# Twelve of sixteen k-tiles of the attention's input products in seven-product form instead of ten

## The chip, the cores and the metric

The kernel runs on one core of one Trainium2 chip. The metric is the device time of one execution in microseconds (us). The kernel before takes 1580.58 us (median of three runs, 1579.58 to 1581.96).

## The reference

A two-layer encoder for 256 tokens of width 2048. Layer 1 is a Mamba-2 mixer. Layer 2 is a forgetting attention with 32 heads of 128. The change touches only the products that make q, k, v and z of layer 2:

```python
def forgetting_attention_mixer(h, w_in, b_forget, w_out):
    proj = h @ w_in                       # h: 256 x 2048
    q = proj[..., :E_WIDTH]               # E_WIDTH = 4096, the same for k, v, z
    ...
    o = o * jax.nn.silu(z)
    return o @ w_out
```

Everything is float32. A float32 product is made of three products of a faster type: each operand is split in a high part and a low remainder, and high*high, high*low and low*high are added up.

## The kernel before, in words

**Splitting the weights.** Each weight tile of 128 x 1024 is loaded (by SP, the engine that issues most loads). ScalarE rounds it into `wh` (`act_hi`, L106), and VectorE subtracts to get the remainder `wl` (`dve_lo`, L112). TensorE multiplies both with the activations (`product`, L132). `prep` (L140) does this for plain weights, `prep_sum` (L172) for weights that are sums. `run` (L209) walks a list of parts. Before the matmuls of a part are emitted, the preparation of the part three places further on (`AHEAD`) is emitted. There are five buffers for `wh`, four for `wl`, and seven (`RAW`) of 128 x 1024 for loaded tiles, the tag `raw`.

**Blocks.** Layer 2 goes over eight groups of four heads (`hq`, `four_heads`, L1136). Each group has two blocks: the first makes q and k, the second v and z. A block multiplies the 256 x 2048 input with a left and a right half of 512 columns. The 2048 rows are 16 k-tiles of 128. With two token tiles, two column halves and pairs of k-tiles, the product is one of 2 x 2 blocks, so it can be made with seven products instead of eight (Winograd's form of Strassen's scheme). This needs sums of the input blocks (`split_form`, L282: seven matrices of 128 x 128 for a pair of k-tiles, held in `forms`) and sums of the weight blocks.

**Sums of weights.** `wf_s` holds, for a set of four k-tiles (two pairs side by side, 128 x 1024), four terms. Three chains run in place. Chain a is term 0, then term 1 is added (A1), then chain b (A3), then term 2 (A2). Chain b is term 3 (B0), then term 1 is added (B1). Chain c is term 2 alone (C0). Each of these seven states is split and multiplied once: six matmuls of 512 columns. Adding a term from memory is done by a DMA that accumulates, issued by GpSimd (POOL, L198). Adding chain b to chain a is done by VectorE (L200).

**What is in sums.** For groups 1 to 7, ten of the sixteen k-tiles (`KS`) are in that form: two sets of four, and a third set of only two k-tiles (`pairs` is 1), 512 wide, from `wf_h`. For the third set, term 1 is loaded once, as `term` (L188, L189), and VectorE adds it to chain a (L196) and to chain b (L193), so one DMA accumulates there, A2. The other six k-tiles are multiplied directly: three tiles `raw` each for the left ("L") and right ("R") columns, twelve matmuls each (`mm_rest`, L1065). Group 0 keeps two sets and four L and four R tiles in each of its blocks, because the forms of the later k-tiles aren't there yet; `late_form` (L952) makes the fifth pair of forms during group 0's second block.

**Order.** `STEPS` (L1019) gives the order of a block of groups 1 to 7: A0 and the other names stand for three parts, one for each set. `FIRST` and `SECOND` are the orders of group 0. After the two blocks of groups 1 to 5 come eight parts (12 matmuls each) of the output projection of the group before (`out_f`, L1355, timed at 22.8 us); the blocks of groups 6 and 7 follow each other without one. The attention of a group itself (transposes, logits, softmax, values) is spread over the parts that follow its second block (`later`, L125).

**Where sums live.** Sums of the first two sets are in `raw` buffers, but chain b of the first set is in a tile `sum` of its own (`apart`). The third set's chains a and b take the sixth buffers of the forms' tags (`gh`, `gl`), changing places from block to block, and c a `raw` buffer. `x3` is the tile that holds k-tiles 10 and 11 of the input; after group 0 the input is still read from `x3` directly by L and R parts. `zth` is a pair of 128 x 512 buffers, used by the gate among others. All instructions of an engine run in the order in which the program lists them, SP's loads and POOL's DMA issues too.

Of the kernel before, what the change touches and what calls it, by code (L numbers as in the profile page):

```python
# [45 lines left out]
KS = 10  # L46
# [23 lines left out]
def hybrid_kernel(ctx: ExitStack, tc: tile.TileContext, a):  # L70
# [101 lines left out]
    def prep_sum(u):  # L172


        name, src, how = u["chain"]
        wide = u.get("wide", 1024)
        if how == "load":
            if u.get("apart"):
                t = fp[0].tile([P, 1024], F32, tag="sum", name=f"sum_{name}")
            elif wide < 1024 and name != "c":  # L180
                t = gp.tile([P, 7, P], F32, tag="gh" if (name == "a") == u["even"] else "gl",
                            name=f"sum_{name}").rearrange("p m s -> p (m s)")
            else:
                t = wp.tile([P, 1024], F32, tag="raw", name=f"sum_{name}", bufs=RAW)
            u["sums"][name] = t[:, :wide]
            nc.sync.dma_start(u["sums"][name], src)
            if wide < 1024 and name == "c":
                u["sums"]["t"] = t = fp[0].tile([P, wide], F32, tag="term", name="term")  # L188
                nc.sync.dma_start(t, u["term"])  # L189
        elif how == "add" and "term" in u:  # L190
            t = u["sums"]["t"]
            if name == "b":
                nc.vector.tensor_tensor(t, t, u["sums"]["b"], op=ALU.add)  # L193
                u["sums"]["b"] = t
            else:
                nc.vector.tensor_tensor(u["sums"][name], u["sums"][name], t, op=ALU.add)  # L196
        elif how == "add":
            behind["POOL"] = nc.gpsimd.dma_start(u["sums"][name], src, accum_op=ALU.add).ins  # L198
        else:
            nc.vector.tensor_tensor(u["sums"][name], u["sums"][name], u["sums"][how], op=ALU.add)  # L200
        raw = u["sums"][name]
        wh = wp.tile([P, 1024], F32R, tag="wh", name="wh")[:, :wide]
        wl = wp.tile([P, 1024], F32R, tag="wl", name="wl", bufs=4)[:, :wide]
        act_hi(wh, raw)
        behind["DVE"] = dve_lo(wl, raw, wh).ins
        u["w"][0] = (wh, wl)
        yield
# [161 lines left out]
    def ktile(x, k):  # L369

        q = max(i for i in range(5) if X_AT[i] <= k)
        return x[q][:, k - X_AT[q]]
# [579 lines left out]
    def late_form():  # L952

        f = fp[0].tile([P, T2, 1024], F32, tag="vz", name="form", bufs=2)
        f = f.rearrange("p t c -> p (t c)")[:, :7 * P].rearrange("p (m s) -> p m s", m=7)
        for i in range(2):
            hi, lo = (ktile(lay2["x"], KS0 + i)[:, j].rearrange("p (t s) -> p t s", t=T2)
                      for j in range(2))
            nc.vector.tensor_tensor(blocks(f, True, i), hi, lo, op=ALU.add)
        split_form(f, True, lay2["forms"], 0, f"x{KS0 // 2}")  # L960
# [58 lines left out]
    STEPS = (A0, C0, "L", B0, "L", A1, "L", A3, "R", "R", "R", B1, A2)  # L1019
    SECOND = (A0, C0, "L", B0, "L", "L", A1, "L", A3, "R", "R", "R", B1, A2, "R")  # L1020
    FIRST = (0, "L", "L", 1, "L", A0, C0, B0, "L", "enter", A1, A3, "R", "R", "R", B1, A2, "R")

    def block_units(w_s, w_p, out, scale, done, order):
# [7 lines left out]
        pairs = (2, 2, 1)[:len(w_s)]  # L1031
        n_l = KT - 2 * len(w_p[0])
        steps = [0]
# [20 lines left out]
        def mm_sum(u, form, name, p2):  # L1054
            wh, wl = u["w"][0]
            first = start(name)
            for i, w in enumerate((wh, wh, wl)):
                for p in range(pairs[p2]):
                    y = lay2["forms"][0][2 * p2 + p][i % 2]
                    product(ps[name], y[:, form, :], w[:, p * 512:p * 512 + 512],  # L1060
                            start=first and i == p == 0,
                            stop=i == 2 and (p2, p + 1) == (len(pairs) - 1, pairs[-1]),
                            skip_group_check=True)
# [31 lines left out]
        for step in order[0]:  # L1095
# [6 lines left out]
            if step in n_rest:  # L1102
                n = n_rest[step]
                n_rest[step] += 1
                names = ("v", "y") if step == "L" else ("z", "u")
                u = us[step]
                parts.append({"u": u, "h": [n],
                              "mm": lambda u=u, n=n, names=names: mm_rest(u, n, names)})
                if n + 1 == len(u["w"]) and step == "L":
                    parts[-1]["post"] = left if order[0] is not SECOND else (  # L1110
                        lambda: [left(), later(1, late_form)])
                continue
            chain, term, how, form, name = step
            for p2 in range(len(pairs)):
                u = {"chain": (chain, w_s[p2][term], how), "sums": sums[p2], "w": [None],
                     "wide": 512 * pairs[p2], "even": order[2],
                     "apart": chain == "b" and p2 == 0 and order[0] is not FIRST}
# [18 lines left out]
    def four_heads(hq, first=()):  # L1136
# [139 lines left out]
        def weights(n):  # L1276
            s1, s2 = a["wf_s"][hq, n], a["wf_h"][hq, n]
            half = lambda c, m: a["wf_p"][hq, n, c][:, m * 1024:m * 1024 + 1024]
            rest = [[half(c, m) for m in range((KT - KS) // 2)] for c in range(2)]
            if hq == 0:  # L1280
                return [s1[0], s1[1]], [[a["wf_b"][n, c], *rest[c]] for c in range(2)]
            return [s1[0], s1[1], s2], rest
# [92 lines left out]
def packed(x, norm_w, m_w_in, m_conv_w, m_conv_b, m_dt_bias, m_A_log, m_D,  # L1375
# [21 lines left out]
    def tiles_b(left, right):  # L1397

        w = np.stack([left.reshape(D, G, 512), right.reshape(D, G, 512)], 2)
        s = w[:KS0 * P].reshape(KS0 // 4, 2, 2, P, G, 2, 512).transpose(4, 0, 2, 5, 3, 1, 6)
        h = w[KS0 * P:KS * P].reshape(2, P, G, 2, 512).transpose(2, 0, 3, 1, 4)
        r = w[KS * P:].reshape(KT - KS, P, G, 2, 512).transpose(2, 3, 1, 0, 4)
        b = w[KS0 * P:KS * P, 0].reshape(2, P, 2, 512).transpose(2, 1, 0, 3)
        return (f(s).reshape(G, KS0 // 4, 4, P, 1024), f(h).reshape(G, 4, P, 512),
                f(r).reshape(G, 2, P, (KT - KS) * 512), f(b).reshape(2, P, 1024))

# [18 lines left out]
    def by_k(w):  # L1428
# [13 lines left out]
        "wf_s": np.stack([qk[0], vz[0]], 1), "wf_h": np.stack([qk[1], vz[1]], 1),  # L1442
        "wf_p": np.stack([qk[2], vz[2]], 1), "wf_b": np.stack([qk[3], vz[3]]),
# [19 lines left out]
```

## Time and profile before

| what | value |
|---|---|
| median of three runs | 1580.58 us |
| the profiled execution: its own time, its span | 1580.13 us, 1578.4 us |
| blocks of group 2 (874.3 to 918.8 and 918.8 to 962.4 us) | 44.5 and 43.6 us |
| the eight output parts behind them (962.4 to 985.2) | 22.8 us |
| blocks of groups 6 and 7 (1317.9 to 1495.1) | 44.5, 43.6, 45.5, 43.6 us |
| POOL, the engine with the least work | 178.1 us (11%) |

The page gives busy times of the engines: PE is TensorE's matmuls, PEld its weight loads, DVE VectorE, ACT ScalarE, POOL GpSimd, SP the engine that issues loads. "DMA share" in a table of stretches is the packet time summed over the core's 16 DMA engines and divided by 16 times the stretch; where two packets overlap on an engine, it can pass 1. A row of a group of instructions has the count, then busy time in us, mean ns of one, and the idle time before them with what ended it.

### The profile page before, as it was taken

The numbers are of one execution on the slowest core, as the hardware profiler recorded it, in microseconds if no ns is written. First come the engines' busy times: TensorE is split into PE (matmuls) and PEld (weight loads), VectorE is DVE, ScalarE is ACT, GpSimd is POOL, SyncE is SP. The second block draws the span as 40 slices with busy tenths as digits, with TensorE's granted clock in tenths as the row PEclk, the third lists the DMA queues.
The fourth block names the chain that finished last, engine by engine and source line by source line (L and its number), as shares of the span: only waits on it lengthen the run. The fifth ranks groups of instructions, "written<-read, shape, count | busy, mean of one in ns | idle before, by whom it ended". The sixth has DMA issues, their size and how long they took to land.

```text
span 1578.4 us, 22860 instructions
## 1 busy us (share of the span) xinstructions
PE 1566.1 (99%) x7768; PEld 1320.7 (84%) x7768; DVE 1377.8 (87%) x2061; ACT 1087.1 (69%) x1710; POOL 178.1 (11%) x225
## 2 busy tenths in 40 slices
PE   9999999999999999999999999999999999999997
PEld 7888888888888888878888888888888888888886
DVE  6998989798989898799888898888888888989886
ACT  7677676767666765766776675776676675777764
POOL 0000111011100110011101110110110111011100
PEclk9999999999999999999999999999999999999999
DMA  9665798769886987579889788788886986899852
GB/s 363 211 204 197 183 275 220 262 177 277 220 271 171 274 227 230 182 170 279 241 250 286 181 239 269 219 230 262 222 262 210 258 271 165 249 276 249 251 175 80
DMA packets 106405, 364.54 MB, mean 231 GB/s; under 512 B 12176, under 2 KB 13072, under 8 KB 106160
## 3 DMA queue, kind: packets, MB, share of 16 engines
q1 hardware_dynamic: 79344, 270.03, 48.5%
q0 software_dynamic: 26800, 92.91, 30.8%
q8 instruction: 61, 1.00, 0.2%
q14 instruction: 56, 0.46, 0.1%
q10 hardware_dynamic: 144, 0.13, 0.0%
HBM read 360.83 MB, written 2.20 MB: 230 GB/s over the span
## 4 chain that ended last, share of the span: by engine, by line
PE 97%; DVE 1%; issue 0%; DMA 0%; ACT 0%; SPq 0%; ACTq 0%; POOLq 0%; POOL 0%
PE psa L132 24%; PE pst L132 17%; PE psx L132 14%; PE psz L132 10%; PE psv L132 9%; PE psu L132 8%; PE psy L132 8%; PE py L715 2%; PE pqk L1182 1%; PE psc L1200 1%; PE ppt L1232 1%; PE po L1258 0%; PE psc L1198 0%; PE pxa L665 0%; PE pyt L778 0%; PE pz L1237 0%
## 5 line engine op out<-in xcount | busy, mean ns | idle before, releaser
L112 DVE TENSOR_TENSOR wl<-raw,wh 128x1024 fp32r<-128x1024 f32 (+2 forms) x343 | 411.8, 1211 | 51.7 <-issue 21.0
L106 ACT ACTIVATE wh<-raw 128x1024 fp32r<-128x1024 f32 (+2 forms) x343 | 356.5, 1052 | 144.0 <-PE psa L132 53.8
L106 ACT ACTIVATE wh<-sum_a 128x1024 fp32r<-128x1024 f32 (+1 forms) x232 | 220.1, 953 | 132.0 <-PE psu L132 36.8
L112 DVE TENSOR_TENSOR wl<-sum_a,wh 128x1024 fp32r<-128x1024 f32 (+1 forms) x232 | 250.2, 1091 | 14.6 <-PE psa L132 5.0
L132 PE MATMUL pst<-x,wh 128*128 128x512 f32 (+1 forms) x800 | 204.3, 396 | 0.9 <-DVE wh L161 0.7
L132 PEld LDWEIGHTS pst<-x,wh 128*128 128x128 f32 (+1 forms) x800 | 145.7, 189 | 30.5 <-ACT x L108 1.4
L132 PE MATMUL psa<-wh,x 128*128 128x512 f32 x512 | 128.7, 391 | 0.0
L112 DVE TENSOR_TENSOR wl<-sum_b,wh 128x1024 fp32r<-128x1024 f32 (+1 forms) x102 | 115.1, 1146 | 5.8 <-ACT wh L106 3.9
L106 ACT ACTIVATE wh<-sum_b 128x1024 fp32r<-128x1024 f32 (+1 forms) x102 | 100.1, 1004 | 26.6 <-PE psa L132 10.5
L132 PEld LDWEIGHTS pst<-x,wl 128*128 128x128 f32 x768 | 106.3, 191 | 9.0 <-DVE wl L112 0.7
L132 PEld LDWEIGHTS psa<-wh,x 128*128 128x128 f32 x512 | 95.5, 188 | 19.7
L132 PE MATMUL pst<-x,wl 128*128 128x256 f32 x768 | 109.3, 283 | 0.0
L198 POOL DMA_DIRECT2D sum_a<-in_wf_s x64 | 55.4, 865 | 407.9 <-DMA raw<-in_wf_p 103.5
L132 PE MATMUL psz<-wh,x 128*128 128x512 f32 x200 | 78.6, 393 | 0.0
L132 PE MATMUL psv<-wh,x 128*128 128x512 f32 x200 | 78.1, 391 | 0.0
L132 PE MATMUL psu<-wh,x 128*128 128x512 f32 x200 | 78.0, 390 | 0.0
L132 PE MATMUL psy<-wh,x 128*128 128x512 f32 x200 | 77.9, 390 | 0.0
L132 PE MATMUL psx<-wh,ghx 128*128 128x512 f32 x234 | 77.7, 399 | 0.0
L106 ACT ACTIVATE wh<-sum_c 128x1024 fp32r<-128x1024 f32 (+1 forms) x58 | 54.5, 954 | 31.8 <-PE psa L132 17.4
L132 PE MATMUL psx<-wh,glx 128*128 128x512 f32 x234 | 75.9, 390 | 0.0
L132 PE MATMUL psx<-wl,ghx 128*128 128x512 f32 x234 | 75.6, 390 | 0.0
L816 DVE TENSOR_TENSOR xs<-psa,xs 128x512 f32<-128x512 f32 (+1 forms) x81 | 51.9, 679 | 22.6 <-PE psa L132 22.2
(365 smaller groups left out, 3390.3 us busy)
## 6 DMA issues: line engine op xcount, KB each, us to landing
raw<-in_wf_p SPq DMA_DIRECT2D x96, 512.0 KB, 5.2
raw<-in_wm_t SPq DMA_DIRECT2D x90, 512.0 KB, 5.1
raw<-in_wm_z SPq DMA_DIRECT2D x64, 512.0 KB, 5.6
sum_a<-in_wf_s POOLq DMA_DIRECT2D x64, 512.0 KB, 8.5
raw<-in_wf_o SPq DMA_DIRECT2D x64, 512.0 KB, 5.8
sum_a<-in_wm_s POOLq DMA_DIRECT2D x36, 512.0 KB, 5.9
sum_a<-in_wf_s SPq DMA_DIRECT2D x32, 512.0 KB, 6.7
sum_c<-in_wf_s SPq DMA_DIRECT2D x32, 512.0 KB, 9.3
```

Of the source, the lines that this page charges most:

```text
L106: nc.scalar.activation(out, in_, AF.Copy)
L112: return nc.vector.tensor_tensor(out, in_, hi.bitcast(F32), op=ALU.subtract)
L132: behind["PE"] = nc.tensor.matmul(*args, **kw).ins
L198: behind["POOL"] = nc.gpsimd.dma_start(u["sums"][name], src, accum_op=ALU.add).ins
L715: nc.tensor.matmul(st["py"][t][:, c], m[:, j, t, :], st["xd"][:, t, c], start=True, stop=True)
L816: nc.vector.tensor_tensor(c, pss[t][:, a:b], c, op=ALU.add)
L1182: nc.tensor.transpose(pt[:, n * P:n * P + P], st["qk"][:, t, c:c + FD], ident)
L1200: nc.tensor.matmul(ps[:, P:P + S], q[:, :P], k[:, P:], start=j == 0, stop=j == 2)
L1232: nc.tensor.transpose(pt[:, c:c + P], uu[:, c:c + P], ident)
```

## The change

The third set gets four k-tiles, as the first two have, so twelve of sixteen k-tiles are in sums for groups 1 to 7, and four are multiplied directly (two L and two R parts).

- All seven states of the third set are 1024 wide, with six matmuls instead of three. Two `raw` tiles (one L, one R) of each block go.
- In the third set term 1 is added to chain a by an accumulating DMA of POOL. To chain b it is added by VectorE, in two instructions of 512 columns, from two tiles (`term` and a `zth` buffer). `wf_h` goes; all sums come from `wf_s`.
- Chain b of the first set returns to the `raw` buffers (except in group 0's second block). The third set's chains a and b live in `x3` and `sum`, changing places from block to block.
- The order of a block becomes A0 C0 B0 L A1 A3 L R R B1 A2.
- `late_forms` makes two more pairs of forms (k-tiles 8 to 11) instead of one. In group 0's second block the last R goes ahead of A2. Group 0's direct tiles are the same in number.

```diff
-KS = 10
+KS = 12
...
         if how == "load":
-            if u.get("apart"):
-                t = fp[0].tile([P, 1024], F32, tag="sum", name=f"sum_{name}")
-            elif wide < 1024 and name != "c":
-                t = gp.tile([P, 7, P], F32, tag="gh" if (name == "a") == u["even"] else "gl",
-                            name=f"sum_{name}").rearrange("p m s -> p (m s)")
+            if "place" in u:
+                t = (bp if u["place"] == "x3" else fp[0]).tile(
+                    [P, 1024], F32, tag=u["place"], name=f"sum_{name}")
             else:
                 t = wp.tile([P, 1024], F32, tag="raw", name=f"sum_{name}", bufs=RAW)
...
+            if "term" in u:
+                u["sums"]["t"] = ts = (fp[0].tile([P, 512], F32, tag="term", name="term"),
+                                       sp.tile([P, 512], F32, tag="zth", name="term"))
+                for i, t in enumerate(ts):
+                    nc.sync.dma_start(t, u["term"][:, i * 512:(i + 1) * 512])
         elif how == "add" and "term" in u:
-            t = u["sums"]["t"]
-            if name == "b":
-                nc.vector.tensor_tensor(t, t, u["sums"]["b"], op=ALU.add)
-                u["sums"]["b"] = t
-            else:
-                nc.vector.tensor_tensor(u["sums"][name], u["sums"][name], t, op=ALU.add)
+            for i, t in enumerate(u["sums"]["t"]):
+                c = u["sums"][name][:, i * 512:(i + 1) * 512]
+                nc.vector.tensor_tensor(c, c, t, op=ALU.add)
...
-    def late_form():
+    def late_forms():
-        f = fp[0].tile([P, T2, 1024], F32, tag="vz", name="form", bufs=2)
-        f = f.rearrange("p t c -> p (t c)")[:, :7 * P].rearrange("p (m s) -> p m s", m=7)
-        for i in range(2):
...
+        v = fp[0].tile([P, T2, 1024], F32, tag="vz", name="form", bufs=2)
+        for q in range(KS0 // 2, KS // 2):
+            f = v[:, q % 2, :7 * P].rearrange("p (m s) -> p m s", m=7)
+            for i in range(2):
...
-    STEPS = (A0, C0, "L", B0, "L", A1, "L", A3, "R", "R", "R", B1, A2)
-    SECOND = (A0, C0, "L", B0, "L", "L", A1, "L", A3, "R", "R", "R", B1, A2, "R")
+    STEPS = (A0, C0, B0, "L", A1, A3, "L", "R", "R", B1, A2)
+    SECOND = (A0, C0, "L", B0, "L", "L", A1, "L", A3, "R", "R", "R", B1, "R", A2)
...
-                for p in range(pairs[p2]):
+                for p in range(2):
...
-                if pairs[p2] == 1 and (chain == "c" or term == 1):
-                    u["term"] = w_s[p2][1]
-                steps[0] += pairs[p2] == 1
-                parts.append({"u": u, "h": [0], "long": 1 if pairs[p2] == 2 else steps[0] % 2,
+                if order[0] is SECOND and chain == "b" and p2 == 0:
+                    u["place"] = "sum"
+                if p2 == 2:
+                    if chain == "c" or (chain, term) == ("b", 1):
+                        u["term"] = w_s[p2][1]
+                    if chain != "c":
+                        u["place"] = "x3" if (chain == "a") == order[2] else "sum"
+                parts.append({"u": u, "h": [0], "long": 1,
```

The host's packing follows: `wf_s` has three sets of four terms for each block, `wf_p` two direct tiles for each column half, `wf_b` k-tiles 8 to 11 for group 0.

More of the change, by code (lines that the diff above doesn't have):

```diff
@@ L175, in prep_sum @@
         name, src, how = u["chain"]
[L176 removed]
         if how == "load":
[L178 to L182 removed]
+            if "place" in u:
+                t = (bp if u["place"] == "x3" else fp[0]).tile(
+                    [P, 1024], F32, tag=u["place"], name=f"sum_{name}")
             else:
                 t = wp.tile([P, 1024], F32, tag="raw", name=f"sum_{name}", bufs=RAW)
[L185 to L189, printed above, removed]
[L190 to L196 removed]
+            u["sums"][name] = t
+            nc.sync.dma_start(t, src)
+            if "term" in u:
[3 more added lines that the diff above has]
+                    nc.sync.dma_start(t, u["term"][:, i * 512:(i + 1) * 512])
+        elif how == "add" and "term" in u:
+            for i, t in enumerate(u["sums"]["t"]):
+                c = u["sums"][name][:, i * 512:(i + 1) * 512]
+                nc.vector.tensor_tensor(c, c, t, op=ALU.add)
         elif how == "add":
@@ L201, in prep_sum @@
         raw = u["sums"][name]
-        wh = wp.tile([P, 1024], F32R, tag="wh", name="wh")[:, :wide]
-        wl = wp.tile([P, 1024], F32R, tag="wl", name="wl", bufs=4)[:, :wide]
+        wh = wp.tile([P, 1024], F32R, tag="wh", name="wh")
+        wl = wp.tile([P, 1024], F32R, tag="wl", name="wl", bufs=4)
         act_hi(wh, raw)
@@ L950, in form_x @@
             split_form(lay2["f"][q], True, lay2["forms"], 0, f"x{q}")
-    def late_form():
-        f = fp[0].tile([P, T2, 1024], F32, tag="vz", name="form", bufs=2)
-        f = f.rearrange("p t c -> p (t c)")[:, :7 * P].rearrange("p (m s) -> p m s", m=7)
-        for i in range(2):
[L957 to L960, printed above, removed]
+    def late_forms():
[3 more added lines that the diff above has]
+            for i in range(2):
+                hi, lo = (ktile(lay2["x"], 2 * q + i)[:, j].rearrange("p (t s) -> p t s", t=T2)
+                          for j in range(2))
+                nc.vector.tensor_tensor(blocks(f, True, i), hi, lo, op=ALU.add)
+            split_form(f, True, lay2["forms"], 0, f"x{q}")
     def stats2():
@@ L1061, in mm_sum @@
                             start=first and i == p == 0,
-                            stop=i == 2 and (p2, p + 1) == (len(pairs) - 1, pairs[-1]),
+                            stop=i == 2 and (p2, p) == (len(w_s) - 1, 1),
                             skip_group_check=True)
@@ L1108, in block_units @@
                               "mm": lambda u=u, n=n, names=names: mm_rest(u, n, names)})
+                if n + 1 == len(u["w"]) and step == "R" and order[0] is SECOND:
+                    parts[-1]["post"] = right
                 if n + 1 == len(u["w"]) and step == "L":
                     parts[-1]["post"] = left if order[0] is not SECOND else (
-                        lambda: [left(), later(1, late_form)])
+                        lambda: [left(), later(1, late_forms)])
                 continue
             chain, term, how, form, name = step
[L1114 to L1117, printed above, removed]
-                if pairs[p2] == 1 and (chain == "c" or term == 1):
-                    u["term"] = w_s[p2][1]
-                steps[0] += pairs[p2] == 1
-                parts.append({"u": u, "h": [0], "long": 1 if pairs[p2] == 2 else steps[0] % 2,
+            for p2 in range(len(w_s)):
+                u = {"chain": (chain, w_s[p2][term], how), "sums": sums[p2], "w": [None]}
+                if order[0] is SECOND and chain == "b" and p2 == 0:
[6 more added lines that the diff above has]
+                parts.append({"u": u, "h": [0], "long": 1,
                               "mm": lambda u=u, form=form, name=name, p2=p2:
@@ L1276, in weights @@
         def weights(n):
-            s1, s2 = a["wf_s"][hq, n], a["wf_h"][hq, n]
-            half = lambda c, m: a["wf_p"][hq, n, c][:, m * 1024:m * 1024 + 1024]
-            rest = [[half(c, m) for m in range((KT - KS) // 2)] for c in range(2)]
+            w_s = a["wf_s"][hq, n]
+            halves = lambda w: [w[:, m * 1024:m * 1024 + 1024] for m in range(2)]
+            rest = [halves(a["wf_p"][hq, n, c]) for c in range(2)]
             if hq == 0:
-                return [s1[0], s1[1]], [[a["wf_b"][n, c], *rest[c]] for c in range(2)]
-            return [s1[0], s1[1], s2], rest
+                return [w_s[0], w_s[1]], [halves(a["wf_b"][n, c]) + rest[c] for c in range(2)]
+            return [w_s[i] for i in range(3)], rest
         return [block_units(*weights(n), out, scale, done,
@@ L1441, in packed @@
         "wm_o": tiles_o(wo)[4 * SUMMED:], "wm_s": tiles_s(wo)[:SUMMED],
[L1442 to L1443 removed]
+        "wf_s": np.stack([qk[0], vz[0]], 1), "wf_p": np.stack([qk[1], vz[1]], 1),
+        "wf_b": np.stack([qk[2], vz[2]]),
         "wf_f": by_k(wf[:, 4 * E:]), "wf_o": tiles_o(wg),
```

11 lines of the change are left out of this document (4 added, 7 removed).

## The prediction

> **What bounds the kernel now.** I read the page first (engines, DMA queues, the chain), then TensorE's own waits, one stretch of the chain, and a table of stretches for the blocks of groups 2, 6 and 7.
>
> ```profile
> span 1578.4 us, 22860 instructions
> ...
> PE 1566.1 (99%) x7768; PEld 1320.7 (84%) x7768; DVE 1377.8 (87%) x2061; ACT 1087.1 (69%) x1710; POOL 178.1 (11%) x225
> ...
> q1 hardware_dynamic: 79344, 270.03, 48.5%
> q0 software_dynamic: 26800, 92.91, 30.8%
> ...
> PE 97%; DVE 1%; issue 0%; DMA 0%; ACT 0%; SPq 0%; ACTq 0%; POOLq 0%; POOL 0%
> ```
> ```profile
> PE warm L132 <- DVE zero L467: 1.6, 1, 1.6
> PE psa L132 <- DVE wl L112: 1.0, 1, 1.0
> PE pst L132 <- DVE wh L161: 0.7, 1, 0.7
> ```
> ```profile
> 863.61 10.89 PE psa L132 x48
> ```
>
> The chain that ended last is TensorE for 97%. A busy share of 99% alone would not say that TensorE never waits, but its waits do: 3.3 us in three places, none of them at a tile of the blocks that change. So layer 2 runs at the pace at which matmuls of 512 columns follow each other: 48 of them in 10.89 us, 0.227 us each. Whatever takes a matmul away there saves 0.227 us, as long as every split weight is still ready in time. The question is what the change does to that readiness, and VectorE and the DMA engines are the two that are nearly full:
>
> ```profile
> 874.30:918.80 44.50, 44.50 (x216) 37.41 (x215) 39.17 (x55) 31.93 (x52) 5.35 (x7) 1.00 0.80 224
> 918.80:962.40 43.60, 43.60 (x208) 36.41 (x207) 38.13 (x50) 32.05 (x47) 6.44 (x8) 1.00 0.91 258
> ...
> 1317.90:1362.40 44.50, 44.50 (x217) 37.42 (x216) 39.17 (x55) 31.82 (x52) 5.41 (x7) 1.00 0.83 227
> 1362.40:1406.00 43.60, 43.60 (x208) 36.44 (x207) 38.15 (x50) 31.87 (x48) 6.52 (x8) 1.00 0.91 253
> 1406.00:1451.50 45.50, 45.50 (x225) 38.33 (x224) 42.32 (x63) 34.15 (x56) 6.90 (x9) 1.00 0.90 247
> 1451.50:1495.10 43.60, 43.60 (x209) 36.42 (x208) 38.39 (x55) 32.39 (x52) 7.10 (x9) 1.00 0.90 251
> ```
>
> The columns are the length, then busy time of PE, PEld, DVE, ACT and POOL, the granted clock (1.00), the DMA share and GB/s. In a block VectorE works 38 to 42 us of 44. Blocks that follow another block directly have a DMA share of 0.90 or 0.91, those that follow output parts 0.80 to 0.83.
>
> **TensorE: the gain.** Before, a block of groups 1 to 7 has 2 x 42 matmuls for the two full sets, 21 for the half set and 72 for six direct tiles, 177. After, it has 3 x 42 + 4 x 12 = 174. Three fewer in each of 14 blocks are 42, at 0.227 us 9.5 us. Group 0's blocks keep their counts. A block of 43.6 us becomes 42.9. TensorE's clock is at 1.00 already, so nothing else can be gained there: 1580.13 - 9.5 = 1570.6 us is the floor.
>
> **VectorE: the price.** The costs of one instruction come from the groups of VectorE in the two blocks of group 2:
>
> ```profile
> L112 DVE TENSOR_TENSOR wl<-sum_a,wh 128x1024 fp32r<-128x1024 f32 x14 | 16.9, 1220 | 0.5 <-PE psz L132 0.2
> ...
> L112 DVE TENSOR_TENSOR wl<-sum_a,wh 128x512 fp32r<-128x512 f32 x7 | 4.8, 686 | 0.8 <-ACT wh L106 0.8
> ...
> L200 DVE TENSOR_TENSOR sum_a<-sum_a,sum_b 128x512 f32<-128x512 f32 x2 | 1.4, 684 | 0.0
> ...
> L193 DVE TENSOR_TENSOR term<-term,sum_b 128x512 f32<-128x512 f32 x1 | 0.7, 684 | 0.0
> L196 DVE TENSOR_TENSOR sum_a<-sum_a,term 128x512 f32<-128x512 f32 x1 | 0.7, 682 | 0.0
> ```
>
> Remainders: 20 x 1.220 + 7 x 0.686 = 29.2 us become 25 x 1.220 = 30.5, 1.30 more. The third set's A3 goes from 0.684 to the 1.220 of a 1024-wide operation, 0.54 more. A1's addition goes to POOL, 0.68 less; B1's becomes two, 0.68 more. Together +1.84 us a block. The v/z block of group 2 then has 38.13 + 1.84 = 40.0 us of work in 42.9, and the one at 1406 has 42.32 + 1.84 = 44.2 in 44.8. All fit, the last barely. The idle time must also be usable, and it is partly waiting by nature:
>
> ```profile
> DVE vz L1050 <- PE psz L132: 12.9, 8, 1.8
> DVE wl L112 <- PE psu L132: 11.7, 8, 1.5
> ```
> ```profile
> 1440.32 0.69 DVE L112 TENSOR_TENSOR wl<-term,wh 128x512 fp32r<-128x512 f32 x1 [1.41 <-PE psu L132]
> ...
> 1442.74 0.75 DVE L1050 SCALAR_TENSOR_TENSOR qk<-psz,rstQ,qk 128x512 f32<-128x512 f32 x1 [1.66 <-PE psz L132]
> ```
>
> In the waits from 760 to 1495 us (total, times, longest) the two largest at the splits are waits of VectorE for TensorE, up to 1.8 and 1.5 us. The two rows of time show them in one block, behind the run of R parts: VectorE is so far ahead that it waits for a `wl` buffer or for a finished accumulation. An ordinary block (1362) idles 43.6 - 38.15 = 5.45 us, 3.3 of it there and 2.15 elsewhere. If both waits stay whole, a block needs 40.0 + 5.45 = 45.45 us, 2.5 more than TensorE. If they shrink to nothing, 42.15, less than 42.9. A wait for TensorE goes away by itself when VectorE falls behind, so I take 0 for ordinary blocks. The block at 1406 needs 44.2 + 2.15 = 46.3 against 44.8, so I take 1.5 us there. It is the place where the margin is thin already:
>
> ```profile
> 1411.90 0.68 DVE L112 TENSOR_TENSOR wl<-sum_c,wh 128x512 fp32r<-128x512 f32 x1
> ```
> ```profile
> 1413.03 0.39 PE L132 MATMUL psv<-wl,ghx 128*128 128x512 f32 x1
> ```
>
> A remainder ready at 1412.58 is read at 1413.03, 0.45 us later. In the new order A3 (two VectorE operations for each 1.36 us of matmuls, so a loss of about 2 x 1.22 - 1.36 = 1.1 us of margin for each of three parts) no longer has an L part (2.72 us of matmuls for one operation) just ahead of it but just behind. The margin is lowest there, and that is where I look for stalls first.
>
> ScalarE has 31.8 to 34.2 us of work in these blocks and gets less than 5 x 1.06 us more, minus the seven short ones; it stays under 40 of 43 and costs nothing.
>
> ```profile
> L106 ACT ACTIVATE wh<-sum_a 128x1024 fp32r<-128x1024 f32 x14 | 14.7, 1055 | 7.4 <-PE psu L132 5.3 <-PE psy L132 1.0 <-PE psz L132 0.8
> ```
>
> **DMA: the other price.** SP's loads are equal in bytes: A0, B0, C0 and `term` of the third set double (four times 256 KB more) and two `raw` tiles of 512 KB go. POOL's accumulates grow by 512 KB (A1, new) and 256 KB (A2, twice as wide), 0.786 MB a block. By the queue rows software DMA takes 0.308 x 1578.4 / 92.91 = 5.2 us of all 16 engines for 1 MB (q1's loads 2.8), so +4.1 us a block. The block at 1362 has 0.91 x 43.6 = 39.7 us of packets, and would have 43.8 in 42.9. The stretches inside it:
>
> ```profile
> 1374.00:1378.00 4.00, 4.00 (x25) 3.48 (x24) 3.87 (x9) 1.96 (x3) 0.00 (x0) 1.00 0.45 137
> 1378.00:1382.00 4.00, 4.00 (x19) 3.34 (x18) 4.00 (x6) 2.83 (x7) 1.19 (x2) 1.00 0.45 62
> ...
> 1390.00:1394.00 4.00, 4.00 (x21) 3.30 (x20) 3.76 (x4) 2.09 (x4) 0.00 (x0) 1.00 1.05 243
> 1394.00:1398.00 4.00, 4.00 (x19) 3.31 (x18) 1.23 (x3) 1.44 (x3) 0.00 (x0) 1.00 1.06 301
> ```
>
> The share goes up to 1.06, so 42.9 us can hold about 45 us of packets, and 8 us in the middle of the block stand at 0.45, 4.4 us free. The new A1 accumulate is issued just ahead of that hole, so it can fill it. What counts is whether data lands in time:
>
> ```profile
> ACT wh L106 <- DMA raw<-in_wf_p: 11.2, 7, 3.0
> ACT wh L106 <- DMA sum_a<-in_wf_h: 2.6, 2, 1.6
> ```
> ```profile
> L198 POOL DMA_DIRECT2D sum_b<-in_wf_s x32: 850/859/892, 697.8 to 1469.7; - x32
> ```
> ```profile
> DMA to landing us min/median/max: 5.4/7.9/13.4
> ```
>
> From 760 to 1495 us ScalarE waits for data of the sums or direct tiles only some 14 us, and none of it reaches TensorE. POOL spends 0.86 us on an issue, and its accumulates land after 5.4 to 13.4 us (1362 to 1495). From A0 of the third set to its A1 TensorE has 7 + 2 parts of 1.36 us and an L of 2.72, 15.0 us; one splitting takes 1.06 + 1.22 us, so a landing within 12 us holds. A2 of the third set is the late one: it lands last of five accumulates in a row, now 2.5 MB rather than 2.25. Between A3 and A2 the order leaves 0.68 us more than before for each of A3 and B1 of the third set, as much as the 0.25 MB cost (1.3 us). I take 0 for the DMA; 2.2 us a block is the other end, if half of the hole can't be used.
>
> [...]
>
> **The hand-over from group 0.** `late_forms` makes one pair of forms more: two sums, four differences and a remainder.
>
> ```profile
> L959 DVE TENSOR_TENSOR form<-x x2: 418/419/420, 728.9 to 729.2; 128x256 f32<-128x256 f32 x2
> ```
> ```profile
> L290 DVE TENSOR_TENSOR form<-form x68: 271/284/293, 121.3 to 732.7; 128x128 f32<-128x128 f32 x68
> ```
> ```profile
> SPq L186 <- DVE wl L112: 173.6, 90, 7.2
> ```
>
> At 2 x 0.42 + 4 x 0.28 + at most 1.22 it is 3.2 us of VectorE, once. The first load into `x3` can't be issued before group 0's R parts have read it; before, that chain had a free buffer. What such a wait can cost lies between 0 and the 7.2 us that a load of a sum waits at most for its buffer. I take 1.0 us.
>
> Sum: 1580.13 - 9.5 + 1.5 + 1.0 = 1573.1 us for the profiled execution. The median is 0.45 us above that execution, so 1573.5.
>
> **The rivals.**
>
> *VectorE takes it back.* Its waits for TensorE shrink only by half, 1.25 us too much in each of eight blocks that follow a block directly (v/z of groups 1 to 7, q/k of group 7), 10 us: 1570.6 + 10 = 1580.6, about 1581. For it: 93% of VectorE's time taken on average. Against it: those waits are behind TensorE and not ahead of it.
>
> *The DMA engines become the bound (slower).* If a packet's time is all that an engine can do in that time (a share of 1.0 and no more) and half of the hole stays empty, a block that follows a block takes 43.8 + 2.2 = 46.0 us instead of 42.9. Eight of those: 1570.6 + 25 = 1595. The place is A2 of the third set, behind five accumulates; it decides once these land later than some 14 us after their issue. For it: shares of 1.05 and 1.06 for 8 us on end. Against it: the hole, and few waits for landings.
>
> *SP's queue is held up.* Four long-lived sums now sit in the seven `raw` buffers rather than three, and the third set's a and b alternate over two single tiles. The second half of `term` needs a `zth` buffer, which the gate uses too. A load that waits for its buffer holds up all loads behind it in SP's order. At 1 us in each of 14 blocks: 1584.6, about 1585. For it: the 173.6 us that sum loads wait on VectorE. Against it: today these waits delay no matmul.
>
> **How the numbers follow.** Something under 0.2% (3.2 us) can't be told from no change. My forecast, at 1570 to 1577.4, has 0.55; VectorE 0.20, mostly within 0.2%; the DMA 0.15 and SP's queue 0.10, both slower. So faster 0.55, same 0.20, slower 0.25. The range starts at 1570, under the floor by its spread of runs, and ends at 1588: it holds the first two cases, SP's queue, and the milder part of the DMA's.
>
> **What would show it.** In the profile after: 42 matmuls fewer; blocks of 42.9 and 43.8 us; VectorE up by 1.8 us a block and its waits for psz and psu shorter; DMA share 0.98 or more in blocks that follow a block, with the stretches at 0.45 filled; TensorE's waits still a few us. Wrong would be: blocks of 44 us or more with TensorE waiting for `wl` at A3 (VectorE), for `wh` of A2 with ScalarE waiting for an accumulate (DMA), or for loads at C0 and B0 (SP's queue).

## The result, and the profile after

The changed kernel takes 1601.99 us (median of four runs, 1601.13 to 1604.31) against 1580.64 us for the kernel before on the same chip: a ratio of 1.0134 [1.0121, 1.0146]. It is slower by 21 us, where 7 us less was forecast, and lies above the range. The profiled execution took 1601.29 us. One execution among all the runs below was slow (the kernel before in the new order, 1953.85 us at a granted clock of 0.753), and that kernel's median leaves it out.

The page of the kernel after, its engines, its two main DMA queues and the head of its chain:

```profile
span 1599.5 us, 22710 instructions
...
PE 1566.1 (98%) x7726; PEld 1313.0 (82%) x7726; DVE 1405.1 (88%) x2040; ACT 1095.5 (68%) x1683; POOL 190.1 (12%) x239
...
q1 hardware_dynamic: 77328, 270.03, 46.1%
q0 software_dynamic: 28816, 103.92, 34.1%
...
PE 6%; issue 0%; DVE 0%; ACT 0%; ACTq 0%; POOLq 0%; POOL 0%
```

The 42 matmuls are gone (7768 to 7726), yet TensorE's busy time is the same 1566.1 us and the span is 21 us longer. The chain, 97% TensorE before, could be followed for 6% only, so it answers nothing here. TensorE's own waits do:

```profile
PE psx L132 <- ACT wh L106: 7.6, 5, 1.5
PE po L1257 <- ACT p L1244: 5.9, 5, 2.1
PE psx L132 <- DVE wl L112: 3.2, 6, 0.7
PE psz L132 <- DVE wl L112: 1.8, 1, 1.8
```

None of these stood in the kernel before. `psx` behind `wh` and `wl` is A3, `po` is the attention of a group. The table of stretches (length, busy time of PE, PEld, DVE, ACT and POOL, clock, DMA share, GB/s) for the blocks of group 2 and the last three blocks tells which blocks pay:

```profile
878.86:922.66 43.80, 43.80 (x213) 36.84 (x212) 41.80 (x56) 32.34 (x50) 5.12 (x6) 1.00 0.88 243
922.66:970.79 48.13, 45.67 (x205) 36.78 (x203) 40.76 (x48) 33.00 (x46) 7.51 (x9) 0.96 0.87 235
1376.81:1422.68 45.87, 44.08 (x204) 35.66 (x203) 40.07 (x47) 30.70 (x43) 7.84 (x10) 1.00 0.89 238
1422.68:1468.29 45.61, 44.46 (x213) 36.43 (x211) 42.08 (x56) 33.15 (x52) 7.08 (x9) 1.00 0.91 259
1468.29:1516.00 47.71, 44.75 (x214) 37.00 (x213) 43.12 (x58) 35.80 (x54) 8.46 (x11) 1.00 0.88 252
```

The q/k block of group 2 fell from 44.48 to 43.80 us, exactly three matmuls of 0.227 us. The v/z block behind it should have taken 42.89 and takes 48.13. All eight blocks that directly follow a block in groups 1 to 7 (v/z of each group, q/k of group 7) are too long; no other is by more than 0.6 us. VectorE works 40 to 43 us in them, as forecast. The DMA share is 0.87 to 0.91, lower than forecast, but only because the blocks are longer: 0.87 of 48.13 us is 41.9 us of packets, which would be 0.98 of 42.89. Both have time left in these blocks, so the first question is what arrives late.

**What is late.** SP's issues of the first L tile's load, in the kernel before and in the kernel after (start, length, number of issues; "SPq" is SP's queue of instructions):

```profile
913.95 0.33 SPq L153 DMA_DIRECT2D raw<-in_wf_p  x1
```
```profile
925.50 2.60 SPq L153 DMA_DIRECT2D raw<-in_wf_p  x3
```

Before, it goes out 4.87 us ahead of its block's start at 918.82. After, it goes out 2.84 us behind the start at 922.66, and three such loads go out together. It waits for a `raw` buffer; the one it gets is that of chain c's first sum, whose splitting ends at 925.47 (three splits of 1.2 us from 924.26, VectorE's timeline):

```profile
924.26 3.48 DVE L112 TENSOR_TENSOR wl<-sum_c,wh 128x1024 fp32r<-128x1024 f32 x3
```

ScalarE does nothing for 5.19 us until that tile has landed, and VectorE waits 4.47 us behind ScalarE. ScalarE's, VectorE's and TensorE's timelines of that block:

```profile
934.26 1.06 ACT L106 ACTIVATE wh<-raw 128x1024 fp32r<-128x1024 f32 x1 [5.19 <-DMA raw<-in_wf_p]
...
945.25 1.06 ACT L106 ACTIVATE wh<-sum_a 128x1024 fp32r<-128x1024 f32 x1 [3.23 <-DVE sum_a L196]
```
```profile
935.62 0.42 DVE L112 TENSOR_TENSOR pl<-ppt,ph 128x256 fp32r<-128x256 f32 x1 [4.47 <-ACT ph L106]
```
```profile
946.33 0.72 PE L132 MATMUL psx<-wl,ghx 128*128 128x512 f32 x2 [0.57 <-DVE wl L112]
...
949.97 0.72 PE L132 MATMUL psx<-wh,ghx 128*128 128x512 f32 x2 [1.51 <-ACT wh L106]
```

The 5 us that ScalarE and VectorE lose at 934 don't stop TensorE at once. They eat the lead, and TensorE stalls 12 to 16 us later, at A3, where the margin is lowest. Who reads only TensorE's waits blames A3 and VectorE. The DMA issues of the trace, put against the starts of the blocks, give the same for all of them:

| first L tile's load | issued, us from its block's start | landed | excess of the block |
|---|---|---|---|
| before, v/z blocks of groups 2 to 6 | -4.87 | -1.25 to -1.11 | none |
| after, q/k blocks of groups 2 to 6 | 2.42 to 2.43 | 7.18 to 8.18 | none |
| after, the eight blocks that follow a block | 2.83 to 4.92 | 10.51 to 13.87 | 1.9 to 5.8 us |

The q/k blocks get their load just as late, but it lands in 4.8 to 5.8 us; in the others it takes 7.7 to 9.0. A landing 8.2 us into the block does no harm here, one at 10.5 does. Both things together make the loss: the late issue and the slow landing. In the block at 922.66 the three loads meet the three accumulates of A1 (issued from 921.08 to 923.97, the last landed at 933.52). After them SP issues no load from 927.77 to 938.51. The DMA share of the two stretches shows both, the crowd and the hole behind it:

```profile
922.66:934.00 11.34, 11.34 (x57) 9.51 (x56) 8.49 (x8) 6.07 (x7) 1.72 (x2) 1.00 1.03 243
934.00:945.00 11.00, 10.74 (x53) 8.89 (x52) 8.63 (x13) 6.54 (x10) 0.86 (x1) 1.00 0.45 118
```

(The excess is against the same block of the kernel `e10` below, the one that loses nothing: 42.9 us for the v/z blocks of groups 2 to 6. It sums to 28.9 us, and the spans of the two differ by 28.5. TensorE's listed waits make 20.0 us of it; the rest stands in the profile as busy time of TensorE. In the v/z blocks of groups 1 and 7 a wait of 2.06 and 1.85 us for the attention lies ahead of the block's own L load. That it is carried over from the late load of the block before is likely, but not shown.)

One more reading: in the block at 1037.44 ScalarE's wait of 4.61 us has another releaser behind it,

```profile
1048.45 1.06 ACT L106 ACTIVATE wh<-raw 128x1024 fp32r<-128x1024 f32 x1 [4.61 <-PE psz L132]
```

but the load issued at 1040.27 landed at 1048.35, 0.1 us before. The 22.4 us that ScalarE's waits list under `raw` are thus too few.

### The profile page after: what moved, and what is told of

It reads as the page before. It is cut to its first block, busy times and chain, and to the rows that moved or that the text cites. A ratio compares the mean times of both kernels' runs of the same rounds, so it can differ in the third digit from the quotient of the medians.

```text
span 1599.5 us, 22710 instructions
## 1 busy us (share of the span) xinstructions
PE 1566.1 (98%) x7726; PEld 1313.0 (82%) x7726; DVE 1405.1 (88%) x2040; ACT 1095.5 (68%) x1683; POOL 190.1 (12%) x239
## 3 DMA queue, kind: packets, MB, share of 16 engines
q0 software_dynamic: 28816, 103.92, 34.1%
## 5 line engine op out<-in xcount | busy, mean ns | idle before, releaser
L112 DVE TENSOR_TENSOR wl<-raw,wh 128x1024 fp32r<-128x1024 f32 (+2 forms) x315 | 378.0, 1209 | 52.3 <-issue 20.1
L106 ACT ACTIVATE wh<-sum_a 128x1024 fp32r<-128x1024 f32 x232 | 242.1, 1058 | 144.1 <-DVE sum_a L196 42.3
L112 DVE TENSOR_TENSOR wl<-sum_a,wh 128x1024 fp32r<-128x1024 f32 x232 | 280.2, 1218 | 14.7 <-ACT wh L106 7.1
L112 DVE TENSOR_TENSOR wl<-sum_b,wh 128x1024 fp32r<-128x1024 f32 x116 | 139.4, 1217 | 10.3 <-ACT wh L106 7.7
L106 ACT ACTIVATE wh<-sum_b 128x1024 fp32r<-128x1024 f32 x116 | 120.9, 1055 | 38.6 <-PE psa L132 10.6
L106 ACT ACTIVATE wh<-sum_c 128x1024 fp32r<-128x1024 f32 x58 | 59.5, 1052 | 24.4 <-PE psa L132 15.2
L132 PE MATMUL psa<-wh,ghf 128*128 128x512 f32 (+1 forms) x260 | 71.0, 392 | 0.0
L132 PE MATMUL psa<-wl,x 128*128 128x512 f32 x256 | 69.2, 390 | 1.0 <-DVE wl L112 1.0
L132 PE MATMUL psa<-wh,glf 128*128 128x512 f32 (+1 forms) x260 | 69.6, 386 | 0.0
L132 PE MATMUL psa<-wl,ghf 128*128 128x512 f32 (+1 forms) x260 | 69.6, 386 | 0.0
```

Of the source, the lines that this page charges most:

```text
L106: nc.scalar.activation(out, in_, AF.Copy)
L112: return nc.vector.tensor_tensor(out, in_, hi.bitcast(F32), op=ALU.subtract)
L132: behind["PE"] = nc.tensor.matmul(*args, **kw).ins
```

## The experiments

The experiments test three theories. LOAD: the first L tile's load is issued too late, because a fourth long-lived sum (chain b of the first set) now takes a `raw` buffer. ORDER: A3 has no L part ahead of it any more. DMA: the larger accumulates fill the DMA engines. Ratios are against executions of the kernel before that were timed together with the run.

**The order of the block.** One L between A1 and A3, in the kernel after:

```diff
-    STEPS = (A0, C0, B0, "L", A1, A3, "L", "R", "R", B1, A2)
+    STEPS = (A0, C0, B0, "L", A1, "L", A3, "R", "R", B1, A2)
```

> The changed kernel with only the order of a block altered: A0 C0 B0 L A1 L A3 R R B1 A2, so an L part stands ahead of A3 again. Theory LOAD (the first L tile's load takes its buffer from chain c's first sum, is issued late and lands late; ScalarE waits 4 to 5 us for it in every v/z block, VectorE behind it 4.5 us, and A3 then has no margin): the wait for the load stays at 4 us, the L ahead of A3 gives back some 1.5 us of margin in each of 8 blocks; 1586 to 1593. Theory ORDER (three A3 parts of two VectorE operations each with no L ahead are too much for VectorE, load or no load): TensorE's idle time at A3 goes, 1573 to 1580. Theory DMA (the engines are full by the added accumulate of A1): as LOAD, at the upper end or no better than 1600.

It takes 1624.05 us, 1.0276 [1.0261, 1.0292]. LOAD's range and ORDER's are both missed, by far; only DMA's open end (no better than 1600) holds it, and `e10` below, which moves the same bytes without the loss, speaks against that theory. TensorE's waits at A3 are gone, as ORDER had it, but the time is lost all the same. The load comes as late as ever (it lands 10.6 to 14.6 us into the v/z blocks of groups 1 to 6), and the stall has moved to the attention:

```profile
PE po L1257 <- ACT p L1244: 19.4, 9, 3.6
```

That it moved because one part less lies between A3 and A2 is likely, but no run tests it. The granted clock explains part of why this run is worse than the kernel after: 0.989 over a span of 1620.2 us against 0.997, which is up to about 13 us (the last section has the clock).

And the other way round, the kernel before with the order of the change:

```diff
-    STEPS = (A0, C0, "L", B0, "L", A1, "L", A3, "R", "R", "R", B1, A2)
+    STEPS = (A0, C0, B0, "L", "L", A1, A3, "L", "R", "R", "R", B1, A2)
```

> The kernel before (ten k-tiles in sums) with the new order as far as it goes: A0 C0 B0 L L A1 A3 L R R R B1 A2. Theory LOAD: it has its own tile for chain b's first set and 2.25 MB instead of 2.5 MB of accumulates in a row, so the order costs little: 1579 to 1584. Theory ORDER: A3 behind A1 without an L between stalls here as well, 1585 to 1600.

It takes 1580.65 us, 1.0003 [0.9994, 1.0013]. A3 without an L ahead of it costs nothing in this kernel, where the load goes out 3.8 us ahead of the v/z blocks. Its third set is still the half one, so this alone doesn't settle ORDER for the changed kernel; `e10` below does, which keeps the new order and loses nothing.

**Less work, at one place or another.** First the new accumulate is left out:

```diff
+        elif how == "add" and "skip" in u:
+            pass
...
+                    if (chain, term) == ("a", 1):
+                        u["skip"] = True
```

> The changed kernel without the accumulate of A1 in the third set (term 1 is left out of that chain): 512 KB of accumulates fewer in each of 14 blocks, all else the same, VectorE's work too. Theory DMA: the first L lands 2.7 us sooner in v/z blocks and most of the loss goes, 1575 to 1585. Theory LOAD: the issue is as late as before, only the landing is shorter; half of the loss goes, 1583 to 1592. Theory ORDER: 1597 to 1602.

It takes 1589.78 us, 1.0050 [1.0034, 1.0066], within LOAD's range. With 0.5 MB a block less to move, nearly half of the loss goes (1.0134 to 1.0050, where `e10` below, without the loss, has 0.9951), but v/z blocks still take 44.5 to 49.1 us, and ScalarE still waits 20.9 us for `raw` loads. SP's loads of L153 (760 to 1480 us) land sooner there, after 6.7 us at the median against 8.2 in the kernel after. So the accumulates have a part in the slow landings; they aren't the whole. Then VectorE's addition at A3 of the third set is left out:

```diff
-        else:
+        elif "skip" not in u:
             nc.vector.tensor_tensor(u["sums"]["a"], u["sums"]["a"], u["sums"]["b"], op=ALU.add)
...
+                    if (chain, term) == ("a", 3):
+                        u["skip"] = True
```

> The changed kernel without VectorE's addition of chain b to chain a in the third set (A3 of that set multiplies the sum as it stood): 1.22 us less VectorE work in each of 14 blocks, right where TensorE idles, loads and DMAs unchanged. Theory LOAD: the late load and ScalarE's 4 us for it stay; the last of the three A3 parts no longer waits for an addition, so part of the idle time goes: 1585 to 1596. Theory ORDER (VectorE's A3 alone is the cause): TensorE's idle time at A3 goes, 1572 to 1580.

It takes 1607.9 us, 1.0161 [1.0145, 1.0177]: no gain at all, a miss for LOAD, which had expected some. ScalarE's and TensorE's timelines of its v/z block from 926.14:

```profile
938.76 1.06 ACT L106 ACTIVATE wh<-raw 128x1024 fp32r<-128x1024 f32 x1 [5.68 <-DMA raw<-in_wf_p]
```
```profile
968.50 0.67 PE L1259 MATMUL po<-p,vz 128*128 128x128 f32 x2 [2.04 <-ACT p L1246]
```

The late load is still there, 12.6 us into the block, and the stall at A3 shrinks (TensorE's waits for `psx` are 3.9 us in place of 10.8); it comes back at the end of the block, where `po` waits 15.0 us in all. Work taken away behind the late load doesn't bring the lost time back. Of the 11.4 us by which this span (1610.9) passes that of the kernel after, up to about 6 are the granted clock, 0.993 against 0.997; why the rest is lost stays open.

Two edits that are alike but for the place: the first, or the second, L tile of each block has no weights of its own and multiplies with those of the part before (one load, one ScalarE and one VectorE operation less). The edit for the first; for the second, `("L", 1)` stands in it:

```diff
+                if order[0] is STEPS and (step, n) == ("L", 0):
+                    other = parts[-1]["u"]
+                    parts.append({"u": u, "h": [], "mm": lambda u=u, n=n, names=names, o=other: [
+                        u["w"].__setitem__(n, o["w"][0]), mm_rest(u, n, names)]})
+                else:
...
```

> The changed kernel where the first L part of groups 1 to 7 has no weights of its own and multiplies with the split weights of the part ahead of it: one load of 512 KB, one ScalarE and one VectorE operation fewer in each of 14 blocks, the matmuls are the same. Theory LOAD: nothing waits for that load any more, TensorE's idle time in v/z blocks under 1 us, 1570 to 1577. Theory ORDER: VectorE is relieved by 1.2 us only, stalls at A3 stay at 1 us or more, 1585 to 1595. Theory DMA: 1.3 us of engine time less of 4.1 added, 1590 to 1597.

> The control to the run in which the first L had no weights of its own: here the second L part of groups 1 to 7 has none and multiplies with the split weights of the part ahead of it. It leaves out the same 512 KB and the same two operations, but behind A3. Theory LOAD: the first L's load is as late as ever, ScalarE waits 4 us for it in v/z blocks, and 1589 to 1600 is measured. If it was the work left out that helped (VectorE or the DMA engines being full), this one gains as much: 1570 to 1577.

Without the first load it takes 1571.82 us, 0.9944 [0.9929, 0.9959], v/z blocks of groups 2 to 6 at 42.89; without the second 1594.77 us, 1.0091 [1.0077, 1.0105], the same blocks at 45.8 to 48.0. ScalarE's waits from 760 to 1520 us, of the first and of the second kernel:

```profile
ACT wh L106 <- DMA sum_a<-in_wf_s: 16.7, 8, 2.7
```
```profile
ACT wh L106 <- DMA raw<-in_wf_p: 30.6, 9, 5.7
ACT wh L106 <- DMA sum_a<-in_wf_s: 10.1, 10, 2.4
```

The work left out is the same; only the place differs, and with it 23 us. So it isn't the amount of work. But this pair can't tell the load from the 1.2 us of VectorE's work that go with it ahead of A3. The next runs can, since they leave nothing out.

**A buffer more.** An eighth `raw` buffer, paid for with the fifth `wh` buffer:

```diff
-RAW = 7
+RAW = 8
...
-        wh = wp.tile([P, 1024], F32R, tag="wh", name="wh")
+        wh = wp.tile([P, 1024], F32R, tag="wh", name="wh", bufs=4)
```

> The changed kernel with eight raw buffers instead of seven, paid for with one of the five wh buffers, in both layers. The first L no longer needs the buffer of chain c's first sum. Theory LOAD: its load is issued 5 us or more sooner, ScalarE's wait for it is under 1 us, TensorE's idle time in v/z blocks under 1 us; 1573 to 1580, unless four wh buffers cost something of their own (seen as ScalarE waiting on TensorE with TensorE idle in layer 1 too). Theory DMA: sooner issues land no sooner in sum, 1593 to 1602. Theory ORDER: 1597 to 1602.

It takes 1578.23 us, 0.9983 [0.9974, 0.9992]. The v/z blocks of groups 2 to 6 are at 42.89. What is lost now lies before these blocks: group 1 starts at 768.87 us instead of 761.81. Four `wh` buffers are one too few for layer 1 and group 0, as the runs that give the fifth back confirm. New among TensorE's waits to 760 us:

```profile
PE psx L132 <- DVE xs L845: 3.6, 3, 1.2
...
PE pk L994 <- DVE lf L986: 1.3, 1, 1.3
```

So the fifth buffer stays `wh` in group 0, and becomes chain b's own from group 1 on, as that chain had before:

```diff
+    made, late = [0], []
...
+    def wh_tile():
+        made[0] += 1
+        if late or made[0] % 5:
+            return wp.tile([P, 1024], F32R, tag="wh", name="wh", bufs=4)
+        return wp.tile([P, 1024], F32R, tag="flex", name="wh", bufs=1)
...
+                if u["place"] == "flex":
+                    late.append(1)
+                    t = wp.tile([P, 1024], F32, tag="flex", name=f"sum_{name}", bufs=1)
...
+                if order[0] is STEPS and chain == "b" and p2 == 0:
+                    u["place"] = "flex"
```

> The changed kernel with a fifth wh buffer that becomes the buffer of chain b's first set from group 1 on; until then it is wh as before, so layer 1 and group 0 keep five wh buffers and seven raw ones, and groups 1 to 7 have four wh buffers and, in effect, eight raw ones. Theory LOAD, and the finding that the run with eight raw and four wh buffers had its v/z blocks at 42.9 us but lost some 6 us in layer 1 and group 0: both go, 1571 to 1574. If four wh buffers cost something in groups 1 to 7 as well, 1575 to 1578.

It takes 1580.81 us, 1.0004 [0.9995, 1.0013], above the 1571 to 1574 that were expected. All is as LOAD has it but for one block, the first of group 1, with 51.22 us:

```profile
776.36 1.22 PE L132 MATMUL psz<-wh,ghx 128*128 128x512 f32 x2 [5.44 <-ACT wh L106]
```

Chain b's first load waits for the buffer until its last `wh` has been read, goes out at 765.82, and holds back the loads behind it: the same fault once more, at the hand-over. The cure is to give the buffer up some parts sooner, at the last B1 of the first set in group 0's second block:

```diff
+        if "last" in u:
+            late.append(1)
...
+                if order[0] is SECOND and (chain, term, p2) == ("b", 1, 0):
+                    u["last"] = True
```

> As the run with the buffer that is wh until group 0 and chain b's after it, but wh gives it up at the last B1 of group 0's second block instead of at the moment chain b asks for it. In that run all blocks but the first of group 1 stood at their floor, and that one idled 5.4 us for chain b's load. Theory LOAD: that idle time goes with an earlier issue, 1571.5 to 1575, under the kernel before by 0.4 to 0.6%. If group 0's end can't do with four wh buffers: 1575 to 1580.

This kernel, `e10`, takes 1572.74 us (1572.19 to 1575.23), 0.9951 [0.9938, 0.9963]. It leaves nothing out and beats both kernels, near the forecast of 1573.5. It has the new order, VectorE's work and the transfers of the change, and only the buffers differ: that is LOAD's strongest proof. Its first L load, the blocks of group 2 (start 873.08 and 916.88) and TensorE's waits from 760 to 1520 us:

```profile
912.23 0.33 SPq L161 DMA_DIRECT2D raw<-in_wf_p  x1
```
```profile
873.08:916.88 43.80, 43.80 (x213) 36.85 (x212) 40.72 (x55) 32.45 (x50) 4.30 (x6) 1.00 0.86 238
916.88:959.77 42.89, 42.89 (x205) 35.84 (x203) 41.64 (x50) 33.38 (x46) 8.37 (x10) 1.00 0.96 257
```
```profile
PE po L1274 <- ACT p L1261: 1.2, 1, 1.2
```

The load is out 4.65 us ahead of the v/z block of group 2, and it lands 0.1 to 1.5 us into the v/z blocks of groups 1 to 6. VectorE has 41.64 us of work in 42.89 and the DMA share is 0.96, and TensorE still doesn't wait. So neither is the bound of the changed kernel.

**The buffer in the kernel before.** Only chain b of the first set goes to `raw`:

```diff
-                     "apart": chain == "b" and p2 == 0 and order[0] is not FIRST}
+                     "apart": chain == "b" and p2 == 0 and order[0] is SECOND}
```

> The kernel before with only chain b's first set moved from its own tile into the raw buffers for groups 1 to 7. Theory LOAD: with one raw buffer less to turn over, loads of L and R tiles come later here too; in the old order an L stands ahead of B0, so that some of the margin is left: 1583 to 1592. Rival: without the wider third set (0.786 MB more a block and 1.8 us of VectorE) a buffer less is harmless, 1580 to 1582.

It takes 1583.77 us, 1.0017 [1.0008, 1.0026]. By itself the lost buffer costs little: of the fourteen blocks only the q/k blocks of groups 1 and 7 grow (45.6 to 46.8 and 45.6 to 48.0 us). With both parts of the change it costs 1.8% (1.0134 against 0.9951). So the loss is not the sum of its parts.

One reason stands in the traces. In this run the first L's load is not late at all: it goes out 4.88 us ahead of the v/z block of group 2, as before. Another load is, that of chain b's second set, which lands 9.7 us into that block, and ScalarE waits for such loads about as long as for the L loads of the kernel after:

```profile
ACT wh L106 <- DMA sum_b<-in_wf_s: 23.6, 9, 5.7
```

Count the `raw` tiles of a block in the order of their loads. Here they are two of A0, three of C0, L, then two of B0: the eighth tile is the second of B0, and the seven buffers are full. In the kernel after B0 stands ahead of L, so the eighth is the first L. In the kernel before with the new order, and in `e10`, chain b's first set has a buffer of its own, L is the seventh, and it goes out 3.8 and 4.7 us ahead. So it takes both the lost buffer and the new order to make the L load late; ORDER, as a theory about VectorE, has fallen, but the order has its part. Why ScalarE's waits of 23.6 us are absorbed here and those of 22.4 us in the kernel after are not (the tile, its place, or the longer landings) stays open, and the changed kernel with its first L ahead of B0 was not run.

**How much DMA room is left.** `e10` with the third set's B1 by an accumulating DMA too, without `term`:

```diff
-                    if chain == "c" or (chain, term) == ("b", 1):
-                        u["term"] = w_s[p2][1]
```

> As the run before it, with the third set's B1 added by an accumulating DMA as well, so that no term is loaded or added by VectorE: 1.37 us less of VectorE, and the six accumulates between A3 and A2 are 3 MB in place of 2.5. If the DMA engines have room once no buffer is short: 1571 to 1576, no different from that run. If they are full: the v/z blocks rise by 1 to 3 us, 1580 to 1600, with ScalarE waiting for accumulates.

It takes 1593.97 us, 1.0082 [1.0068, 1.0096], as was expected if the DMA engines are full. VectorE is relieved of two operations a block, and 21 us are lost. In its block from 919.37 the six accumulates go out between 935.29 and 944.35; ScalarE, then TensorE:

```profile
954.63 1.06 ACT L106 ACTIVATE wh<-sum_b 128x1024 fp32r<-128x1024 f32 x1 [6.62 <-PE psx L132]
```
```profile
959.13 0.58 PE L1271 MATMUL po<-pl,vhl 128*128 128x256 f32 x1 [1.67 <-DVE pl L112]
```

The wait for `sum_b` (put down to `psx`, but it is the tile that the accumulates write) takes 6.6 us: that accumulate went out at 941.85 and landed at 954.52. The DMA share is 1.04 from 940 to 950 us and 1.03 from 950 to 960, and the longest landing of an accumulate is 17.4 us rather than 14.8. DMA is the next bound: here one accumulate more is too much. (Of the 21 us up to about 6 are the granted clock, 0.994 against 0.998.)

## Why the prediction was wrong

- **TensorE's gain: right.** The q/k blocks of groups 2 to 6 lost 0.68 us each, and the span of `e10` is 7.4 us shorter than before's, where 9.5 of gain less 2.5 of losses were forecast.
- **VectorE's price: right.** 27.3 us more work in all (1405.1 against 1377.8) are measured, where 14 x 1.84 + 3.2 = 29 was forecast. That ordinary blocks would bear it was right too, as `e10` shows. The 1.5 us for the tight block, q/k of group 7, were not lost there: it takes 43.72, under the forecast floor of 44.8, because matmuls of the attention have moved to the block behind it (the profile has 213 there for 225, and 214 for 209 in the block behind). The two blocks together take 89.2 us, 0.1 more than before where three matmuls fewer in each should have made it 1.4 less. So 1.5 us are lost, but TensorE's wait there is 1.2 us in the later block, for the attention (`po` behind ScalarE's `p`) and not for a split of VectorE. That the size fits is luck.
- **DMA: bytes right, time too high.** Software DMA costs 0.341 x 1599.5 / 103.92 = 5.2 us a MB as before. But the loads, with equal bytes in fewer packets, fell from 0.485 x 1578.4 = 766 to 0.461 x 1599.5 = 737 us, so the blocks got 2.2 us more packets each instead of 4.1. The share of 0.98 was not reached (0.96 in `e10`). The hole of 0.45 in the middle of the block was to be filled by the new accumulate of A1; in the kernel after that one goes out and lands ahead of it, and the hole stays.
- **The step that failed: "I take 0 for the DMA", in a sum that also has nothing for a load held up in SP's queue within a block.** Measured, this term is 28.9 us, and the forecast missed the profiled execution by 28.2 (1601.3 against 1573.1). The step looked at whether the accumulates A1 and A2 land in time, and took for granted that loads are issued when they were. The first L's load was the one to follow: its buffer's last reader decides when it can start, and that had moved 7.7 us. The row needed, SP's timeline around a block's start, was never read.
- **The rival "SP's queue is held up" had the mechanism**, four long-lived sums in seven buffers, and the stated sign. It failed in its price: 1 us in each of 14 blocks came from no row. It is 1.9 to 5.8 us in eight. "Today these waits delay no matmul" was no argument, since the wait in question didn't exist in the kernel before.
- **The place was half right, and the reading of it would have misled.** Stalls were forecast at A3, for `wl`, as a sign of VectorE. Of TensorE's 20.0 us of waits 10.8 came there, 7.6 of them for `wh` and 3.2 for `wl`, for a cause 12 us earlier; 5.9 came at the attention. Of the other places named for SP's queue, C0 shows none and B0 one, 1.8 us in the v/z block of group 1.
- **The hand-over from group 0: nothing of the 1.0 us is seen in `e10`.** Group 1 starts at 762.46 us there (762.30 before), and its two blocks take 1.4 us less, the six matmuls. The 51.22 us above came from an edit of the study.
- **That `e10` comes so near to 1573.5 is in part luck:** it is another kernel than the one forecast, one loss of the sum came at another place and the other not at all.

## What to carry to other kernels

When a change moves a long-lived tile into a ring of buffers, count for each load that uses the ring how many tiles lie ahead of it, work out which reader frees its buffer and when, before and after, and compare that with the landing time, not only with the need for the data. Here TensorE's stall came 12 to 16 us behind its cause: follow the engine ahead of it back to its last wait for a DMA. And a buffer may be worth more in one phase than in another; let it change its role, but early enough for its first load.

## What the runs showed of the hardware

In the kernel after, up to 1590 us of its span, the granted clock leaves 1.00 once, behind a stall. In the block at 922.66 TensorE waits 0.57 and 1.51 us within 3.7 us, and then (stretches of the kernel after, then single matmuls):

```profile
945.00:950.00 5.00, 2.92 (x13) 1.75 (x11) 4.97 (x8) 3.99 (x9) 2.58 (x3) 1.00 0.80 131
950.00:955.50 5.50, 5.38 (x16) 3.94 (x16) 5.25 (x6) 5.26 (x7) 1.60 (x2) 0.69 1.04 202
```
```profile
952.38 0.63 PE L132 MATMUL psy<-wh,x 128*128 128x512 f32 x1
952.81 0.63 PE L132 MATMUL psv<-wh,x 128*128 128x512 f32 x1
```

The granted clock is 0.69, and matmuls follow each other by 0.43 us instead of 0.227, seven or eight of them, some 1.6 us on top of the stall. Four other blocks with stalls of 1.50 to 1.54 us at the same place show no such stretch.

The clock of 0.50 lasts from 951.72 to 955.13 us, 3.41 us. In stretches of that length, counted from there, this stall and that of the block at 1037.44 look so:

```profile
948.31:951.72 3.41, 1.78 (x7) 1.06 (x7) 3.13 (x5) 3.03 (x5) 0.61 (x2) 1.00 1.05 198
951.72:955.13 3.41, 3.41 (x10) 2.63 (x9) 3.41 (x4) 3.41 (x4) 1.40 (x2) 0.50 1.05 205
1060.95:1064.36 3.41, 1.87 (x9) 1.24 (x8) 3.38 (x6) 2.73 (x8) 1.53 (x2) 1.00 0.94 139
1064.36:1067.77 3.41, 3.29 (x14) 2.37 (x14) 3.16 (x3) 3.41 (x5) 1.60 (x2) 1.00 1.00 198
```

TensorE idles 1.63 us of the first stretch, and the clock is 0.50 in the next. It idles 1.54 us of the third, and the clock stays at 1.00. It stays as well behind a stall that does not come from A3, the wait of 2.06 us for the attention at 810.06, and there TensorE idles more, 1.70 us of such a stretch:

```profile
808.36:811.77 3.41, 1.71 (x11) 1.58 (x12) 3.41 (x5) 2.61 (x4) 0.92 (x2) 1.00 1.08 261
811.77:815.19 3.42, 3.42 (x17) 2.83 (x16) 3.42 (x8) 2.79 (x4) 0.00 (x0) 1.00 1.06 220
```

So the idle time of one stretch, read from the matmul records, doesn't tell the fall from the stalls without one. What brings the clock down is not shown, and no run was made to test it.
